# Storing a decoder block's result in pieces of 64 tokens instead of 32, and summing the first weights on GpSimd

## The chip, the cores and the metric

The kernel runs on one core of a Trainium2 chip. A core has TensorE (matmuls), VectorE, ScalarE and GpSimd, each with its own instruction stream, and SyncE (SP), which only issues DMAs; ScalarE can issue DMAs as well. In a profile they are PE (PEld for its weight loads), DVE, ACT, POOL and SP; SPq and ACTq are the issuing parts of two of them. Work on different engines is ordered by semaphores alone. The metric is the device time of one execution in microseconds, the median of several runs.

## What is computed

One block of a decoder for 512 tokens of width 2048 in float32: RMSNorm, one projection whose columns feed three token mixers (dilated attention, a convolution module, windowed attention), an output projection with residual, and then a SwiGLU feed-forward with residual:

```python
x = x + mix @ w_out[l]
h2 = _rms_norm(x, norm2_g[l])
x = x + (jax.nn.silu(h2 @ w_gate[l]) * (h2 @ w_up[l])) @ w_down[l]
```

The feed-forward is 5632 wide. The change lies in it alone.

## The kernel before

Every matrix product is done in three passes of a rounded type: each operand is split into a high half (rounded, on ScalarE) and a low half (the rest, on VectorE), and high x high, high x low and low x high are added. Gate and up (class `Wide`, 22 pairs of feature tiles) and down (class `Down`) also use a fast scheme for 2 x 2 blocks with seven products instead of eight, so that sums of weight blocks and sums of activation blocks have to be made.

*Weights.* A group of four blocks "11", "12", "21", "22" of gate and up is loaded by SP into raw buffers. `group` lists four additions per group (`add`, L184): s = 21 + 22, 21 += 11, s += 11, s += 12, each done in place once the split that reads the old value has been issued. They run on GpSimd, but for the very first group, g0, whose sums run on VectorE. `split_up_to` then makes the halves, two products ahead: two ScalarE copies (L295 into PSUM, L296 the high half) and a VectorE subtraction (L267). Down's weights are split the same way at L283 to L285, with the blocks rearranged in eight runs of 128 as they are written.

*Activations for down.* `Wide.piece` splits a result for 256 tokens per product: a ScalarE copy (L1154) into columns 0 to 255 of a tile `a` and a VectorE subtraction (L1155) into the next 256. The tile goes to DRAM and is loaded again for down. In `Down`, 128 of these columns at a time are TensorE's stationary operand, so that columns 0 to 127 (a = 0) and 128 to 255 (a = 1) give two output tiles [128 tokens, 512 channels].

*Down.* Twelve blocks (`DOWN`), g alternating between the halves of the output channels; each has seven products, each in two steps. The partial sums `y` carry a key (g, i, k, a): channels 1024 i + 512 g on, tokens 256 k + 128 a on. `done` adds the products to them; blocks 10 (g = 1) and 11 (g = 0) are the last of their half. The order of the work around it is written by hand in two lists, `evacs` and `extras`: `later(n, ...)` puts a call n steps ahead, and each step runs the front of both. The program runs on each engine in that order.

*Results.* The output is wanted with channels in rows. `store` (L1241 to L1259) transposes a finished `y` tile in 32 x 32 blocks on VectorE (L1245) into a tile `zo` and issues four DMAs, one for each 32 partitions (L1252): 32 rows of 16 pieces of 32 tokens, 128 bytes a piece. All are on SP's queue, except in the last product of all (`tail` in `product`), which is cut into a = 0 and two halves of a = 1, whose stores alternate between SP and ScalarE's queue. Stores that stand in `extras` when the tail begins are issued after it, in the closing loop. The residual is loaded through `turned` in the same arrangement of tokens.

The framework gives DMAs of SP and ScalarE's queue eight completion semaphores in turn (DMAHW0 to 7 in the lists below); a DMA waits for the one that used its semaphore before.

Of the kernel before, what the change touches and what calls it, by code (L numbers as in the profile page):

```python
# [9 lines left out]
F32 = mybir.dt.float32  # L10
# [6 lines left out]
P = 128  # L17
# [99 lines left out]
def kernel(ctx: ExitStack, tc: tile.TileContext, xT, wi, wo, wgu, wd, cst_in, outT):  # L117
# [51 lines left out]
    def group(name, m, n, blocks):  # L169

        key = {k: (k, name) for k in ("11", "12", "21", "22", "s")}
        for k in ("22", "21", "11", "12"):
            entries.append((k + "ab"[m] if k[0] == "2" else k, key[k], blocks[k]))
        u = len(works)

        def add(to, a, b, last=None):
            def go():
                if to == a:
                    out = raws[key[to]][0]
                else:  # L180
                    out = take("s" + "ab"[m], key[to], n)

                eng = nc.vector if name == "g0" else nc.gpsimd
                eng.tensor_add(out[:, :n], raws[key[a]][0][:, :n], raws[key[b]][0][:, :n])  # L184
                if last:
                    drop(key[last])
            return go

        sums[u - 4].append(add("s", "21", "22"))
        sums[u - 3].append(add("21", "21", "11"))  # L190
        sums[u].append(add("s", "s", "11", "11"))
        sums[u + 2].append(add("s", "s", "12"))
        works.extend((key[k], last, None) for k, last in (
            ("s", False), ("11", False), ("21", True), ("s", False), ("12", True), ("22", True), ("s", True)))
# [15 lines left out]
    for t, (g, r) in enumerate(DOWN):  # L210
        first, end = RANGES[r]
        base = len(works)
        keys, size = {}, {}
        for c, (lo, hi) in {"A": (first, first + 2), "B": (first + 2, end)}.items():
            keys[c] = {k: (k, f"d{t}{c}") for k in ("11", "12", "21", "22", "s")}
            size[c] = 4 * P * (hi - lo)
            bufs[c]["12"] = bufs[c]["11"]
        for k in ("21A", "11A", "21B", "11B", "22A", "22B", "12A", "12B"):
            c = k[2]
            span = (first, first + 2) if c == "A" else (first + 2, end)  # L220
            entries.append((bufs[c][k[:2]], keys[c][k[:2]], [down_block(g, int(k[0]) - 1, int(k[1]) - 1, *span)]))

        def add(c, other, last=False, buf=None):
            key, n = keys[c], size[c]

            def go():

                out = raws[key["21"]][0] if buf is None else take(buf, key["s"], n)
                nc.gpsimd.tensor_add(out[:, :n], raws[key["21"]][0][:, :n], raws[key[other]][0][:, :n])
                if last:  # L230
                    drop(key[other])
            return go

        for i, c in enumerate("AB"):
            sums[base - 4 + i].append(add(c, "11", buf=bufs[c]["s"]))
            sums[base + i].append(add(c, "22"))
            sums[base + 3 + i].append(add(c, "11", last=True))
            sums[base + 7 + i].append(add(c, "12"))
        works.extend((keys[c][k], last, "moves") for k, last in (
            ("s", True), ("11", False), ("21", False), ("21", False), ("22", True), ("12", True), ("21", True)) for c in "AB")  # L240
        bufs = {c: {"21": b["s"], "s": b["11"], "11": b["22"], "22": b["21"]} for c, b in bufs.items()}

    splits = {}
# [797 lines left out]
    acts = {}  # L1041
    od = {p: tc.dram_tile([P, 7 * T], F32, name=f"od{p}") for p in range(NP)}
    evacs, extras = [], []
    flip = [1]

    def run(queue):
# [44 lines left out]
    class Wide(Block):  # L1091
# [55 lines left out]
        def piece(self, at, src):  # L1147
            n = src.shape[-1] // TH
            near = psum["high"].tile([P, 1024], F32R, name=f"{self.name}n{at}", tag="h")[:, :n * TH]
            nc.scalar.copy(near, src)  # L1150
            for k in range(n):
                q, s = LAID[at + k], slice(k * TH, (k + 1) * TH)
                t = slot(f"a{q}_{self.p}", F32R)
                nc.scalar.copy(t[:, :TH], src[:, s])  # L1154
                nc.vector.tensor_sub(t[:, TH:], src[:, s], near[:, s].bitcast(F32))  # L1155
                later(0, nc.sync.dma_start, od[self.p][:, (at + k) * T:(at + k + 1) * T], t.bitcast(F32), queue=extras)

        def piece1(self):
# [19 lines left out]
    def turned(dram, key, part):  # L1178

        g, i, k, a = key  # L1180
        c, t = 1024 * i + 512 * g, 256 * k + P * a + 32 * part
        return dram[c:c + T, t:t + 32].rearrange("(b i) t -> i b t", i=32)

    def by_blocks(t, part):
# [53 lines left out]
                load_next(3)  # L1238
            run(extras)

    def store(key, lo=0, hi=T, engs=(nc.sync,), now=False):  # L1241

        g, i, k, a = key
        z = slot("zo")
        nc.vector.transpose(z[:, lo:hi], y[key][:, lo:hi])  # L1245

        def go():
            out = outT.rearrange("n p t -> (n p) t")
            for part in range(4):
                c = 1024 * i + 512 * g  # L1250
                to = out[c + lo:c + hi, 256 * k + P * a + 32 * part:256 * k + P * a + 32 * part + 32]
                engs[part % len(engs)].dma_start(to.rearrange("(b i) t -> i b t", i=32),  # L1252
                                                 z[32 * part:32 * part + 32, lo:hi].rearrange("p (b j) -> p b j", j=32))
        if now:
            go()
        else:
            later(1, go, queue=extras)
        if hi == T:
            y.pop(key)  # L1259

    class Down:

# [9 lines left out]
        def product(self, k, q):  # L1272
# [13 lines left out]
            if tail:  # L1286

                out = banks + outs[:1]
                for n, (a, lo, hi) in enumerate(((0, 0, T), (1, 0, TH), (1, TH, T))):
                    self.multiply(q, out[n], units, a, lo, hi, True, True)  # L1290
                    key = self.sum(0, 1, a)
                    s = y[key][:, lo:hi]
                    nc.vector.tensor_add(s, s, out[n][:, lo:hi])
                    store(key, lo, hi, (nc.sync, nc.scalar), now=True)
                    if n == 0:
                        for b in range(2):
                            store(self.sum(0, 0, b), now=True)
                return
            if self.drops:
                for j in self.pairs:  # L1300
# [21 lines left out]
        def done(self, q, banks):  # L1322
            by = nc.vector
            for a, b in enumerate(banks):
# [12 lines left out]
                elif q == 4:  # L1337
                    self.add(1, 0, a, b, by)
                    if self.end:
                        later(0, store, self.sum(1, 1, a))  # L1340
                elif q == 2 and self.end:

                    t = slot(f"last{a}")
                    nc.scalar.copy(t, b)
                    self.add(0, 0, a, t, nc.gpsimd)
                    store(self.sum(1, 0, a))
                elif q == 2:
                    self.add(0, 0, a, b, by)
                else:
# [6 lines left out]
            if q == 3 and self.final:  # L1356
                for n, (i, k) in enumerate(((0, 0), (1, 1), (1, 0), (0, 1))):
                    for a in range(2):
                        later(2 * n + a, store, self.sum(i, k, a))

    blk = gate = None
    for t in range(len(DOWN)):
# [88 lines left out]
```

## Time and profile before

| | |
|---|---|
| median of 3 runs | 1904.18 us (1904.1 to 1905.18) |
| profiled execution, its own time | 1905.0 us |
| its span, first to last instruction | 1903.1 us |
| TensorE busy | 1874.6 us, 99% of the span |
| VectorE, ScalarE, GpSimd busy | 1466.9, 1347.0, 1057.3 us |
| stores of the result | 62 on SP, 6 on ScalarE's queue |

Rows of a timeline or group read: start and length in us (or busy and mean), engine, line, operation, output <- inputs, shape, count, and in brackets the idle time before it with what ended it. "SPq L1252 <- DMA out_T<-zo: 16.4, 4, 15.1" is a wait: who, for whom, us in total, times, longest. A window's row gives its length, each engine's busy time with the number of instructions, TensorE's granted clock, the mean busy share of the 16 DMA engines and GB/s.

### The profile page before, as it was taken

The numbers are of one execution on the slowest core, as the hardware profiler recorded it, in microseconds if no ns is written. First come the engines' busy times: TensorE is split into PE (matmuls) and PEld (weight loads), VectorE is DVE, ScalarE is ACT, GpSimd is POOL, SyncE is SP. The second block draws the span as 40 slices with busy tenths as digits, with TensorE's granted clock in tenths as the row PEclk, the third lists the DMA queues.
The fourth block names the chain that finished last, engine by engine and source line by source line (L and its number), as shares of the span: only waits on it lengthen the run. The fifth ranks groups of instructions, "written<-read, shape, count | busy, mean of one in ns | idle before, by whom it ended". The sixth has DMA issues, their size and how long they took to land.

```text
span 1903.1 us, 28403 instructions
## 1 busy us (share of the span) xinstructions
PE 1874.6 (99%) x9718; PEld 1603.6 (84%) x9718; DVE 1466.9 (77%) x2472; ACT 1347.0 (71%) x1869; POOL 1057.3 (56%) x662
## 2 busy tenths in 40 slices
PE   9999999999999999999999999999999999999994
PEld 7888888888888888888888888888888888888884
DVE  6789978998678777777778777777777777777774
ACT  6356654553467888888788888888788778777772
POOL 0111101000002887888787887887787878878773
PEclk9999999999999999999999999999999999999997
DMA  7232242333332445555456555554448857657435
GB/s 267 95 123 77 84 132 77 109 122 133 124 131 106 133 166 155 166 186 160 165 157 191 167 178 156 167 183 159 156 140 310 313 200 238 217 200 258 154 112 88
DMA packets 218785, 307.11 MB, mean 161 GB/s; under 512 B 80912, under 2 KB 130448, under 8 KB 218640
## 3 DMA queue, kind: packets, MB, share of 16 engines
q1 hardware_dynamic: 216352, 305.02, 49.5%
q8 instruction: 77, 1.26, 0.3%
q10 hardware_dynamic: 2288, 0.27, 0.1%
q14 instruction: 68, 0.56, 0.1%
HBM read 243.89 MB, written 52.95 MB: 156 GB/s over the span
## 4 chain that ended last, share of the span: by engine, by line
PE 96%; DVE 1%; POOL 1%; DMA 1%; issue 0%; ACT 0%; SPq 0%; DVEq 0%; POOLq 0%
PE out L1076 45%; PE out L1311 7%; PE out L1312 7%; PE out L1310 7%; PE o L318 3%; PE o L319 3%; PE o L320 3%; PE cq L320 2%; PE cq L318 2%; PE cq L319 2%; PE av L318 1%; PE ak L318 1%; PE av L320 1%; PE aq L320 1%; PE aq L318 1%; PE ak L320 1%
## 5 line engine op out<-in xcount | busy, mean ns | idle before, releaser
L1076 PE MATMUL out<-h,wh 128*128 128x512 f32 x2464 | 589.4, 391 | 0.0
L1076 PEld LDWEIGHTS out<-h,wh 128*128 128x128 f32 x2464 | 453.4, 189 | 87.7
L1076 PEld LDWEIGHTS out<-h,wl 128*128 128x128 f32 x2464 | 316.6, 192 | 14.2 <-DVE n2v L433 2.2
L1076 PE MATMUL out<-h,wl 128*128 128x256 f32 x2464 | 320.6, 283 | 2.0 <-DVE n2v L433 2.0
L1311 PE MATMUL out<-wl,a 128*128 128x512 f32 x620 | 241.1, 389 | 0.4 <-DVE wl L285 0.4
L1312 PE MATMUL out<-wh,a 128*128 128x512 f32 x620 | 240.4, 388 | 0.0
L1310 PE MATMUL out<-wh,a 128*128 128x512 f32 x620 | 240.4, 388 | 0.0
L289 ACT CAST wh<-w 128x1024 fp32r<-128x1024 f32 (+2 forms) x94 | 96.7, 1030 | 123.4 <-PE o L319 54.6
L267 DVE TENSOR_TENSOR wl<-w,wh 128x1024 fp32r<-128x1024 f32 (+2 forms) x95 | 112.8, 1187 | 37.2 <-ACT wh L289 37.0
L1311 PEld LDWEIGHTS out<-wl,a 128*128 128x128 f32 x620 | 116.4, 188 | 26.3 <-DVE wl L285 2.5
L1310 PEld LDWEIGHTS out<-wh,a 128*128 128x128 f32 x620 | 116.4, 188 | 24.2
L1312 PEld LDWEIGHTS out<-wh,a 128*128 128x128 f32 x620 | 116.4, 188 | 23.5
L1320 DVE TENSOR_TENSOR y<-y,out 128x512 f32<-128x512 f32 x164 | 106.3, 684 | 32.9 <-PE out L1312 20.8
L529 DVE SCALAR_TENSOR_TENSOR y<-bu,cst,y 128x511 f32<-128x511 f32 (+14 forms) x120 | 87.6, 730 | 0.4
L434 POOL TENSOR_TENSOR n2r<-n2v,nhalf 128x4 f32<-128x4 f32 x1 | 2.0, 2030 | 109.5 <-DVE n2v L433 109.5
L318 PE MATMUL o<-mh_c,wh 128*128 128x512 f32 x128 | 51.1, 399 | 0.0
L318 PE MATMUL cq<-hh,wh 128*128 128x512 f32 x128 | 51.1, 399 | 0.0
L320 PE MATMUL cq<-hh,wl 128*128 128x512 f32 x128 | 50.1, 391 | 0.0
L320 PE MATMUL o<-mh_c,wl 128*128 128x512 f32 x128 | 50.0, 391 | 0.0
L319 PE MATMUL cq<-hl,wh 128*128 128x512 f32 x128 | 50.0, 390 | 0.0
L319 PE MATMUL o<-ml_c,wh 128*128 128x512 f32 x128 | 49.9, 390 | 0.0
L434 POOL TENSOR_TENSOR lvr<-lvv,nhalf 128x4 f32<-128x4 f32 x1 | 1.9, 1921 | 74.5 <-DVE lvv L433 74.5
(3012 smaller groups left out, 4935.1 us busy)
## 6 DMA issues: line engine op xcount, KB each, us to landing
od<-a SPq DMA_DIRECT2D x154, 256.0 KB, 4.8
a<-od SPq DMA_DIRECT2D x154, 256.0 KB, 5.4
w<-in_wi SPq DMA_DIRECT2D x58, 512.0 KB, 3.6
w<-in_wo SPq DMA_DIRECT2D x32, 512.0 KB, 3.5
x<-in_xT SPq DMA_DIRECT2D x16, 256.0 KB, 6.9
xr<-in_xT SPq DMA_DIRECT2D x16, 256.0 KB, 3.7
x2d<-xr SPq DMA_DIRECT2D x16, 256.0 KB, 2.0
z<-x2d SPq DMA_DIRECT2D x64, 64.0 KB, 3.7
```

The source lines that it names most:

```text
L267: fn(*args)
L289: (nc.vector.tensor_copy if u == 0 else nc.scalar.copy)(hi[:, :n], t[:, :n])
L318: nc.tensor.matmul(out, wh, xh, start=start, stop=False)
L319: nc.tensor.matmul(out, wh, xl, start=False, stop=False)
L320: nc.tensor.matmul(out, wl, xh, start=False, stop=stop)
L434: nc.gpsimd.tensor_tensor(r, v, nhalf[:, :NT], op=ALU.pow)
L529: nc.vector.scalar_tensor_tensor(yconv[j][:, i:], hconv[j][:, :T - i], c, yconv[j][:, i:], op0=ALU.mult, op1=ALU.add)
L1076: nc.tensor.matmul(out, lhs[:, s], rhs, start=begin, stop=x is xs[-1] and low == flip[0], skip_group_check=True)
L1310: nc.tensor.matmul(b[:, lo:hi], x[:, high], wh[:, s], start=start, stop=False, skip_group_check=True)
L1311: nc.tensor.matmul(b[:, lo:hi], x[:, high], wl[:, s], start=False, stop=False, skip_group_check=True)
L1312: nc.tensor.matmul(b[:, lo:hi], x[:, low], wh[:, s], start=False, stop=last, skip_group_check=True)
L1320: getattr(eng, op)(t, t, src)
```

## The change

It has three parts. The tokens of a 256-token group are dealt to the two tiles in turns of 32: tile a takes tokens 64 b + 32 a + j for b = 0 to 3 and j = 0 to 31, so L1154 and L1155 write and read eight runs of 32 (`by_turns`, `by_tiles`), and the residual is loaded accordingly. The two tiles' transposes then write side by side into one tile per pair (`turn_back`), and one DMA for each 32 partitions stores 64 tokens in a piece, 256 bytes (`put`). These tiles take buffers of weights that the last block has used up. Third, g0's sums move to GpSimd.

```diff
@@ add in group
-                eng = nc.vector if name == "g0" else nc.gpsimd
-                eng.tensor_add(out[:, :n], raws[key[a]][0][:, :n], raws[key[b]][0][:, :n])
+                nc.gpsimd.tensor_add(out[:, :n], raws[key[a]][0][:, :n], raws[key[b]][0][:, :n])
...
+        final_bufs = bufs
         bufs = {c: {"21": b["s"], "s": b["11"], "11": b["22"], "22": b["21"]} for c, b in bufs.items()}
...
+    def by_turns(x):
+        return x.rearrange("p (b a j) -> p b a j", a=2, j=32)
+
+    def by_tiles(x):
+        return x.rearrange("p (a b j) -> p b a j", a=2, j=32)
@@ Wide.piece
-                nc.scalar.copy(t[:, :TH], src[:, s])
-                nc.vector.tensor_sub(t[:, TH:], src[:, s], near[:, s].bitcast(F32))
+                nc.scalar.copy(by_tiles(t[:, :TH]), by_turns(src[:, s]))
+                nc.vector.tensor_sub(by_tiles(t[:, TH:]), by_turns(src[:, s]), by_turns(near[:, s].bitcast(F32)))
@@ turned
-        c, t = 1024 * i + 512 * g, 256 * k + P * a + 32 * part
+        c, t = 1024 * i + 512 * g, 256 * k + 64 * part + 32 * a
@@ in place of store
+    pairs_out, engines = {}, [nc.sync, nc.scalar]
+
+    def turn_back(key, lo=0, hi=T):
+        g, i, k, a = key
+        if (g, i, k) not in pairs_out:
+            c = "AB"[len(pairs_out) % 2]
+            name = "22" if g == i == 0 else "s"
+            pairs_out[g, i, k] = wp.tile([P, 1024], F32, name=f"z{g}{i}{k}", tag=f"raw{final_bufs[c][name]}", bufs=1)
+        z = pairs_out[g, i, k].rearrange("p (b a j) -> p a b j", a=2, j=32)[:, a, lo // 32:hi // 32]
+        nc.vector.transpose(z, y[key][:, lo:hi].rearrange("p (b j) -> p b j", j=32))
         if hi == T:
             y.pop(key)
+
+    def put(g, i, k, lo=0, hi=T, engs=(nc.sync,)):
+        out, z = outT.rearrange("n p t -> (n p) t"), pairs_out[g, i, k]
+        c = 1024 * i + 512 * g
+        for part in range(4):
+            to = out[c + lo:c + hi, 256 * k + 64 * part:256 * k + 64 * part + 64]
+            engs[part % len(engs)].dma_start(to.rearrange("(b i) t -> i b t", i=32),
+                                             z[32 * part:32 * part + 32, 2 * lo:2 * hi].rearrange("p (b j) -> p b j", j=64))
@@ Down.product, the tail
-                    store(key, lo, hi, (nc.sync, nc.scalar), now=True)
+                    if n == 0:
+                        put(self.g, 1, 0)
...
+                    turn_back(self.sum(0, 1, a), lo, hi)
                     if n == 0:
                         for b in range(2):
-                            store(self.sum(0, 0, b), now=True)
+                            turn_back(self.sum(0, 0, b))
+                        put(self.g, 0, 0, engs=engines)
+                    else:
+                        put(self.g, 0, 1, lo, hi, engines)
@@ Down.done
-                        later(0, store, self.sum(1, 1, a))
+                        later(0, turn_back, self.sum(1, 1, a))
...
-                    store(self.sum(1, 0, a))
+                    turn_back(self.sum(1, 0, a))
+                    if a == 0:
+                        put(self.g, 1, 1)
...
-                        later(2 * n + a, store, self.sum(i, k, a))
+                        later(2 * n + a, turn_back, self.sum(i, k, a))
+                    later(2 * n + 2, put, self.g, i, k, queue=extras)
```

TensorE's list of instructions is the same, word for word. GpSimd's list around the start of gate and up, before (lvr and n2r are small steps of two norms):

```order
L434 TENSOR_TENSOR lvr<-lvv,nhalf 128x4
L434 TENSOR_TENSOR n2r<-n2v,nhalf 128x4
L184 TENSOR_TENSOR w('s', 'u0')_6059<-w('21', 'u0')_5736,w('22', 'u0')_5734 128x1024
L184 TENSOR_TENSOR w('21', 'u0')_5736<-w('21', 'u0')_5736,w('11', 'u0')_5984 128x1024
L1109 TENSOR_TENSOR g0r<-g0r,g0u 128x256
```

and with the change:

```order
L433 TENSOR_TENSOR lvr<-lvv,nhalf 128x4
L182 TENSOR_TENSOR w('s', 'g0')_5681<-w('21', 'g0')_5527,w('22', 'g0')_5525 128x1024
L182 TENSOR_TENSOR w('21', 'g0')_5527<-w('21', 'g0')_5527,w('11', 'g0')_5581 128x1024
L182 TENSOR_TENSOR w('s', 'g0')_5681<-w('s', 'g0')_5681,w('11', 'g0')_5581 128x1024
L433 TENSOR_TENSOR n2r<-n2v,nhalf 128x4
L182 TENSOR_TENSOR w('s', 'g0')_5681<-w('s', 'g0')_5681,w('12', 'g0')_5684 128x1024
L182 TENSOR_TENSOR w('s', 'u0')_6059<-w('21', 'u0')_5736,w('22', 'u0')_5734 128x1024
```

Three of g0's sums stand ahead of n2r, the fourth between n2r and the sums of the next group.

SP's list at its end, before. The first two rows are the last of the store ahead of the wait that the prediction speaks of, then come the eight held stores of g = 1, of which the first five are shown, and the first of the tail's own; 13 more of the tail's and 16 of earlier keys follow:

```order
L1252 DMA out_T<-zo 32x16x32 [waits DMAHW7_49]
L1252 DMA out_T<-zo 32x16x32 [waits DMAHW2_49]
L1252 DMA out_T<-zo 32x16x32 [waits DMAHW3_49,DVE_49]
L1252 DMA out_T<-zo 32x16x32 [waits DMAHW4_49]
L1252 DMA out_T<-zo 32x16x32 [waits DMAHW5_49]
L1252 DMA out_T<-zo 32x16x32 [waits DMAHW6_49]
L1252 DMA out_T<-zo 32x16x32 [waits DMAHW7_49,DVE_49]
...
L1252 DMA out_T<-zo 32x16x32 [waits DMAHW3_49,DVE_49]
```

and SP's whole list from the last pair but three on with the change (z_19027 is the pair i = 1, k = 1 of g = 0, z_19051 is 1, 0, z_19080 is 0, 0 and z_19078 is 0, 1):

```order
L1268 DMA out_T<-z_19027 32x16x64 [waits DMAHW2_49]
L1268 DMA out_T<-z_19051 32x16x64 [waits DMAHW4_49,DVE_49]
L1268 DMA out_T<-z_19051 32x16x64 [waits DMAHW7_49]
L1268 DMA out_T<-z_19051 32x16x64 [waits DMAHW1_49]
L1268 DMA out_T<-z_19051 32x16x64 [waits DMAHW2_49]
L1268 DMA out_T<-z_19080 32x16x64 [waits DMAHW3_49,DVE_49]
L1268 DMA out_T<-z_19080 32x16x64 [waits DMAHW4_49]
L1268 DMA out_T<-z_19078 32x8x64 [waits DMAHW5_49,DVE_49]
L1268 DMA out_T<-z_19078 32x8x64 [waits DMAHW6_49]
L1268 DMA out_T<-z_19078 32x8x64 [waits DMAHW7_49,DVE_49]
L1268 DMA out_T<-z_19078 32x8x64 [waits DMAHW0_49]
```

ScalarE's list at its end with the change:

```order
L1358 COPY last_19057<-out_5942 128x512 [waits PE_49]
L1268 DMA out_T<-z_19080 32x16x64 [waits DMAHW7_49,DVE_49]
L1268 DMA out_T<-z_19080 32x16x64 [waits DMAHW1_49]
L1268 DMA out_T<-z_19078 32x8x64 [waits DMAHW3_49,DVE_49]
L1268 DMA out_T<-z_19078 32x8x64 [waits DMAHW5_49]
L1268 DMA out_T<-z_19078 32x8x64 [waits DMAHW6_49,DVE_49]
L1268 DMA out_T<-z_19078 32x8x64 [waits DMAHW0_49]
```

The semaphores are dealt in one sequence over both lists: 7 goes to ScalarE's first store and then to the second store of z_19051, 1 to ScalarE's second and then to the third, 3 to ScalarE's third and then to the first store of z_19080, and so on to the end. Before, 3 went to ScalarE's second store and then to the third row of SP's list above.

More of the change, by code (lines that the diff above doesn't have):

```diff
@@ L1239 @@
             run(extras)
-    def store(key, lo=0, hi=T, engs=(nc.sync,), now=False):
+    pairs_out, engines = {}, [nc.sync, nc.scalar]
+    def turn_back(key, lo=0, hi=T):
         g, i, k, a = key
[L1244 to L1257, printed above, removed]
+        if (g, i, k) not in pairs_out:
[4 more added lines that the diff above has]
+        nc.vector.transpose(z, y[key][:, lo:hi].rearrange("p (b j) -> p b j", j=32))
         if hi == T:
             y.pop(key)
+    def put(g, i, k, lo=0, hi=T, engs=(nc.sync,)):
[5 more added lines that the diff above has]
+                                             z[32 * part:32 * part + 32, 2 * lo:2 * hi].rearrange("p (b j) -> p b j", j=64))
     class Down:
@@ L1290, in product @@
                     self.multiply(q, out[n], units, a, lo, hi, True, True)
-                    key = self.sum(0, 1, a)
-                    s = y[key][:, lo:hi]
-                    nc.vector.tensor_add(s, s, out[n][:, lo:hi])
-                    store(key, lo, hi, (nc.sync, nc.scalar), now=True)
+                    if n == 0:
+                        put(self.g, 1, 0)
+                    t = y[self.sum(0, 1, a)][:, lo:hi]
+                    nc.vector.tensor_add(t, t, out[n][:, lo:hi])
+                    turn_back(self.sum(0, 1, a), lo, hi)
                     if n == 0:
                         for b in range(2):
-                            store(self.sum(0, 0, b), now=True)
+                            turn_back(self.sum(0, 0, b))
+                        put(self.g, 0, 0, engs=engines)
+                    else:
+                        put(self.g, 0, 1, lo, hi, engines)
                 return
```

## The prediction

> **What bounds the kernel now.** I read the chain of waits first, then the last 40 us of each queue's timeline, then the one idle stretch of TensorE. The chain:
>
> ```profile
> PE 96%; DVE 1%; POOL 1%; DMA 1%; issue 0%; ACT 0%; SPq 0%; DVEq 0%; POOLq 0%
> ```
>
> TensorE sets the pace of nearly everything, and the change leaves its instructions as they are. So only time in which TensorE does not run can be won: the end, and a gap. The end, from the timelines of TensorE, VectorE and the two issuing queues, SP's waits, the account of the store's line and a window on the stores alone (columns there: length, busy of the five engines, clock, DMA share, GB/s):
>
> ```profile
> 1878.17 0.28 PE L1312 MATMUL out<-wh,a 128*128 128x256 f32 x1
> 1872.07 1.29 DVE L1245 STREAM_TRANSPOSE zo<-y 128x512 f32<-128x512 f32 x2
> 1876.41 1.90 DVE L1245 STREAM_TRANSPOSE zo<-y 128x512 f32<-128x512 f32 x3
> 1879.44 0.45 DVE L1245 STREAM_TRANSPOSE zo<-y 128x256 f32<-128x256 f32 x1
> 1877.16 3.88 ACTq L1252 DMA_DIRECT2D out_T<-zo  x6
> 1855.92 8.47 SPq L1252 DMA_DIRECT2D out_T<-zo  x14
> 1879.58 21.11 SPq L1252 DMA_DIRECT2D out_T<-zo  x38
> 1892.04 8.65 SPq L1252 DMA_DIRECT2D out_T<-zo  x16
> SPq L1252 <- DMA out_T<-zo: 16.4, 4, 15.1
> DMA to landing us min/median/max: 1.6/2.0/4.3
> 1892.00:1900.00 8.00, 0.00 (x0) 0.00 (x0) 0.00 (x0) 0.00 (x0) 0.00 (x0) 0.50 0.73 112
> ```
>
> TensorE ends at 1878.45 and VectorE's last transpose at 1879.89, but the span ends at 1903.1. In between SP issues 38 stores one after the other, 21.11 / 38 = 0.556 us each, and the last landing and the program's end take the 2.4 us from 1900.69 to 1903.1. Issue is the bound there: the DMA engines are busy for 0.73 of the window. Before that SP stood still for 15.1 us, from 1864.4 to 1879.5, held by a DMA of the same line: each issue first waits for the DMA that last used its completion semaphore (eight of them, shared by SP and ScalarE's queue), and the store on which SP stood has the semaphore of ScalarE's second tail store, which could not start before the last sums. SP went on 2.4 us after ScalarE's first store: half a microsecond of issue and a landing of 2.0. So eight stores of results long ready were held there, the tail's own 14 came behind them, and then 16 more of ready results.
>
> The gap, in the timelines of TensorE, ScalarE, VectorE and GpSimd around the start of gate and up:
>
> ```profile
> 603.31 1.11 PE L1076 MATMUL out<-h,wl 128*128 128x256 f32 x8
> 606.39 1.92 PE L1076 MATMUL out<-h,wl 128*128 128x256 f32 x8 [1.97 <-DVE n2v L433]
> 600.18 0.40 ACT L975 CAST h<-h 128x256 fp32r<-128x256 f32 x1
> 603.99 1.02 ACT L295 CAST wn<-w('s', 'g0')_5681 128x1024 fp32r<-128x1024 f32 x1 [3.41 <-DVE w('s', 'g0')_5681 L184]
> 586.31 1.22 DVE L267 TENSOR_TENSOR wl<-w('s', 'g0')_5681,wn 128x1024 fp32r<-128x1024 f32 x1
> 601.61 1.22 DVE L267 TENSOR_TENSOR wl<-w('21', 'g0')_5527,wn 128x1024 fp32r<-128x1024 f32 x1
> 602.74 1.22 DVE L184 TENSOR_TENSOR w('s', 'g0')_5681<-w('s', 'g0')_5681,w('11', 'g0')_5581 128x1024 f32<-128x1024 f32 x1
> 605.04 1.22 DVE L267 TENSOR_TENSOR wl<-w('s', 'g0')_5681,wn 128x1024 fp32r<-128x1024 f32 x1 [1.08 <-ACT wn L295]
> 606.42 2.03 POOL L434 TENSOR_TENSOR n2r<-n2v,nhalf 128x4 f32<-128x4 f32 x1 [109.48 <-DVE n2v L433]
> 608.42 2.39 POOL L184 TENSOR_TENSOR w('s', 'u0')_6059<-w('21', 'u0')_5736,w('22', 'u0')_5734 128x1024 f32<-128x1024 f32 x1
> 614.28 1.01 ACT L295 CAST wn<-w('s', 'u0')_6059 128x1024 fp32r<-128x1024 f32 x1
> ```
>
> TensorE stands for 1.97 us. The row names n2v, but what its product needs is the low half that VectorE finishes at 606.26, just before n2v. That waits for ScalarE's rounding at 603.99, which waited 3.41 us for VectorE's sum of 602.74. The sum stands in VectorE's order behind the work of the output projection. GpSimd sat idle for 109 us.
>
> **The change, part by part.** Sums are made against the profiled execution: span 1903.1, own time 1905.0, which is 0.8 above the median of 1904.18; I take the same saving off the median.
>
> *Sums of the first gate group to GpSimd.* Four additions leave VectorE. The one that matters has its operands when VectorE has read the first s, at 587.5; on GpSimd such a sum takes 2.39 us, so it is done by 590, ten us before ScalarE, free at 600.58, wants it. Then ScalarE rounds at 600.6 to 601.6, VectorE goes from 601.61's row straight to this low half and ends at about 604.0, and TensorE has its last matmul before the gap running until then. The 1.97 us go: **-2.0**. What is late next: GpSimd's fourth sum, queued between n2r and u0's first sum. Both start 2 us earlier, since n2v does, so u0's sum would end near 611.2, where it now ends at 610.8. ScalarE reads it at 614.3 now and 612.3 then; 1.1 us are left. Bounds: nothing (another wait takes over) to -2.2.
>
> *Pieces of 64 tokens.* A store now carries 32 rows x 16 pieces of 256 bytes, not 128. For all 68 stores of before (62 on SP, six on ScalarE's queue) there are now 36: 30 on SP, six on ScalarE's queue. Before, 38 of SP's came after 1879.5. By the new order 21 precede the first one that shares a semaphore with ScalarE's tail stores: four pairs of g = 1 and, as sums become ready, pair (1,1) and the first store of (1,0). All have data by about 1873.4, when the two transposes of 1872.07 end, and leave while TensorE works. Nine are left. The first of them waits for the landing of ScalarE's first tail store. That one follows the third transpose, whose end is 1878.31, so it goes at 1878.35 and lands 2.0 us later, at 1880.35. Nine issues at 0.556 take 5.0: the last issue ends at 1885.35, where it ended at 1900.69. The other stores of ScalarE's queue that these nine also wait for go at about half a microsecond's distance and land before SP's turn (the sixth at some 1883.5, SP's ninth being due at 1884.8). Saved: **-15.3**.
>
> What a 256-byte piece costs has no row. Issue: the rows with 512 pieces of 128 bytes take 0.55 us. If issue goes by pieces it stays at that; if by bytes it doubles to 1.1. Below nothing is excluded, since a store has no fewer pieces. I take 0.556. On the DMA engines a store now takes 0.73 x 0.55 = 0.40 us; after, 0.40 (by pieces) to 0.80 (by bytes). Seven full and eight half stores fall into the tail, 11 full ones' worth, 4.4 to 8.8 us against 7.0 from ScalarE's first store to SP's last issue. Between the two: gate and up moves 168 GB/s at a share of 0.53 (row below), 317 at a full one, in pieces of kilobytes; at that rate 64 KB take 0.20, which leaves 0.20 for 512 short pieces, so 128 KB in as many take 0.41 + 0.20 = 0.61. Eleven are 6.7 us: the engines just keep up, and I leave the sum to issue.
>
> The Trainium skill ("DMA: Bandwidth & Descriptors", section "Why small descriptors are slow (HBM only)") gives a descriptor a fixed overhead of 3 cycles beside one for every 32 bytes. By that rule 256 bytes cost 11 cycles and 128 cost 7, an estimate of 0.63 us a store, 6.9 us in all; the sum would stay as it is, only just. The same page (section "Issuing engines are not separate DMA queues") speaks against the second queue: several issuers save only the sequencer's time, which it calls usually small. Here the trace disagrees with "small": 0.55 of issue against 0.40 of engine. By the rule ScalarE's six stores would save nothing; fifteen in one file from 1878.35 would end at 1886.7, and the sum would be 1.3 us worse.
>
> *Transposes.* They write 16 runs of 32 now. No row shows this; the nearest are two lines of the down stage that write eight runs of 128, beside a plain copy and 605.04's plain subtraction of the same size:
>
> ```profile
> L283 ACT CAST wn<-w('21', 'd0A')_14842 x3: 1005/1010/1022, 1462.5 to 1483.4; 128x1024 fp32r<-128x1024 f32 x3
> L295 ACT CAST wn<-w('s', 'g0')_5681 x3: 1007/1017/1020, 582.3 to 612.4; 128x1024 fp32r<-128x1024 f32 x3
> L285 DVE TENSOR_TENSOR wl<-w('21', 'd0A')_14842,wn x3: 1214/1214/1222, 1465.0 to 1485.4; 128x1024 fp32r<-128x1024 f32 x3
> ```
>
> Runs cost nothing there, so I take 0; the bound is twice the time, +1.9 for the three on the path. A gain has no source.
>
> *Copies by turns.* 154 roundings on ScalarE (L1154) and 154 subtractions on VectorE (L1155) now read and write eight runs of 32. By the same rows: 0. Cover, in a stretch of gate and up, for all engines and for L1154 alone:
>
> ```profile
> 700.00:1400.00 700.00, 700.00 (x4028) 618.73 (x4027) 534.15 (x790) 580.18 (x738) 560.72 (x360) 1.00 0.53 168
> 700.00:1400.00 700.00, 45.59 (x126) 1.00 0.53 168
> ```
>
> ScalarE is idle for 119.8 us, 0.95 per copy of 0.36; VectorE for 165.9. Without that cover 0.1 us more per copy would cost 15 us.
>
> *The reused buffers.* The results' tiles now take the place of finished weights, each used twice or thrice, so a transpose waits for stores, and behind it on VectorE stand low halves for TensorE. The tightest is pair (0,1) of g = 1, behind pair (1,1)'s stores, which now come after the second load of 12:
>
> ```profile
> 1853.71 0.76 SPq L252 DMA_DIRECT2D w('12', 'd11B')_18875<-in_wd  x1
> 1859.83 0.69 DVE L1245 STREAM_TRANSPOSE zo<-y 128x512 f32<-128x512 f32 x1
> ```
>
> The load goes some 0.6 us earlier than now, the four stores after it are issued by about 1855.8 and land by 1857.8, or 1859.6 at the longest landing seen (4.3 from issue). The transpose comes at 1859.83: 0.
>
> Sum: -2.0 - 15.3 = -17.3: span 1885.8, own time 1887.7, median **1886.9**.
>
> **Rivals.** *Bytes decide on the DMA engines* (0.80 a store). 8.8 us from 1878.35 end at 1887.15, where the forecast's issue ends at 1885.35: 1.8 later, 1888.7. For it: no row shows pieces of 256 bytes. Against: the 317 GB/s of large pieces beside the 112 / 0.73 = 153 of short ones; by bytes alone they would be equal.
>
> *Bytes decide at issue*, 1.1 us each: nine stores end 5 us later, 1891.9. Against: the load of 512 KB at 1853.71 was issued in 0.76.
>
> *The gap stays*, because ScalarE or GpSimd is late with something else: 1888.9. Against: the 10 us of slack of the sum.
>
> *The change does not free SP.* The shared semaphores hold all 14 stores of the last four pairs, not nine: five more at 0.556, 1889.7. For it: exactly this stood for 15.1 us. Against: the new order's waits name long landed stores for these five.
>
> *Slower: the copies by turns make ScalarE the bound of gate and up.* Place: L1154, 154 copies. It decides from 0.36 + 0.95 = 1.31 us a copy on; 0.11 us beyond that, 1.42, eats the whole gain. At four times the price, 1.45, it costs 0.14 x 154 = 21.6 and gives 1908.5. For it: eight short runs per copy, twice over. Against: the L283 row, which has as many runs and no cost.
>
> **How the numbers follow.** Forecast 0.66 (1885 to 1888.3: transposes, landings and the engines' share). Engines by bytes 0.13, gap stays 0.08, SP held again 0.05, issue by bytes 0.03, slower 0.02; the rest, 0.03, is a tail shorter than I reckon, because landings are quicker or the issue of fewer rows is. The range 1884.4 to 1890.8 takes in all but the last two rivals and the ends of the unknown costs. Faster by more than 0.2% (3.8 us; about what can be told from no change): all but the slower case and a percent or two of mishaps in it, 0.96; same 0.02, slower 0.02.
>
> **What would show it.** Right: SP's row of out_T stores after TensorE's end has 9, not 38, at 0.55 each, the first 2.0 us after ScalarE's first; the span ends about 9.3 us after TensorE's last matmul, where it was 24.7. TensorE's wait of 1.97 at the third product's successor is gone and its last matmul ends near 1876.4. L1154 keeps its 0.36 us. Wrong: a DMA share near 1 in the tail (engines by bytes), 1 us between issues (issue by bytes), ScalarE over 95% in gate and up (slower), a wait of VectorE's transposes for out_T, or more than nine stores behind ScalarE's first.

## The result and the profile after

The changed kernel takes 1886.51 us (median of 5 runs, 1886.18 to 1886.97), beside 1904.1 us for the kernel before on the same chip (1903.15 to 1905.18): a ratio of 0.9908, 95% interval 0.9893 to 0.9922. That is 17.6 us less; the forecast was 17.3 less. The profiled execution took 1886.69 us, its span 1884.7, which is 18.4 less than the span before. The sum came out well because two terms missed in opposite directions, so the two places are shown apart.

First the end of the span, from the timelines of TensorE, VectorE, ScalarE's queue and SP in the changed kernel (start, length, engine, line):

```profile
1874.17 0.28 PE L1326 MATMUL out<-wh,a 128*128 128x256 f32 x1
1872.41 1.90 DVE L1258 STREAM_TRANSPOSE z<-y 128x512 f32<-128x512 f32 x3
1875.43 0.45 DVE L1258 STREAM_TRANSPOSE z<-y 128x256 f32<-128x256 f32 x1
1874.34 3.01 ACTq L1268 DMA_DIRECT2D out_T<-z  x6
1876.75 5.64 SPq L1268 DMA_DIRECT2D out_T<-z  x9
```

TensorE ends at 1874.45 and the span at 1884.7. These 10.25 us, which I call the tail, were 24.65 before and 9.3 in the forecast. SP has nine stores behind ScalarE's first, as foretold. But the first of them comes 2.41 us after ScalarE's first, not 2.0, and the nine take 0.63 us each, not 0.556. SP's waits, the stores' times to landing and a window on the nine stores (length, busy time of five engines, clock, share of the DMA engines, GB/s) say why:

```profile
SPq L1268 <- DMA out_T<-z: 7.0, 2, 6.7
```

```profile
out_T<-z ACTq DMA_DIRECT2D x2, 128.0 KB, 2.5
out_T<-z ACTq DMA_DIRECT2D x4, 64.0 KB, 2.1
```

```profile
1876.70:1882.40 5.70, 0.00 (x0) 0.00 (x0) 0.00 (x0) 0.00 (x0) 0.00 (x0) 0.65 0.99 188
```

A store of 128 KB lands in 2.5 us where one of 64 KB takes 2.1; the forecast had used the 2.0 of the 64 KB stores of before. And the DMA engines are busy for 0.99 of the window: at 188 GB/s a store of 128 KB takes 0.70 us of theirs. In this stretch they are the bound, and no longer the issue. SP still stands for 6.7 us, held by ScalarE's first tail store.

Second the start of gate and up, in the timelines of TensorE, ScalarE, VectorE and GpSimd with the change:

```profile
603.18 2.07 PE L1083 MATMUL out<-h,wl 128*128 128x256 f32 x16
605.09 2.00 PE L1083 MATMUL out<-h,wh 128*128 128x512 f32 x8
606.93 0.60 PE L366 MATMUL r2s<-ident,n2r 128*128 128x128 f32 x4
600.35 1.01 ACT L294 CAST wn<-w('s', 'g0')_5681 128x1024 fp32r<-128x1024 f32 x1
602.60 1.22 DVE L266 TENSOR_TENSOR wl<-w('s', 'g0')_5681,wn 128x1024 fp32r<-128x1024 f32 x1
587.53 2.45 POOL L182 TENSOR_TENSOR w('s', 'g0')_5681<-w('s', 'g0')_5681,w('11', 'g0')_5581 128x1024 f32<-128x1024 f32 x1 [16.77 <-DVE wl L266]
607.32 2.40 POOL L182 TENSOR_TENSOR w('s', 'u0')_6059<-w('21', 'u0')_5736,w('22', 'u0')_5734 128x1024 f32<-128x1024 f32 x1
```

The sum starts at 587.53 on GpSimd, ScalarE rounds at 600.35, VectorE's low half ends at 603.82 and TensorE does not stand. All this is as forecast. Yet the small transposes of r2s, which came 7.53 us after the start of the first of these matmuls (603.31 to 610.84), now come 3.75 us after it: 3.8 us are gone where the gap was 1.97. The kernel before has a second loss there that I had not read. Two windows of its trace, the first one with the gap in it:

```profile
603.23:606.64 3.41, 1.44 (x12) 1.20 (x11) 2.31 (x4) 2.65 (x3) 0.22 (x1) 0.99 0.43 132
606.64:610.05 3.41, 3.41 (x13) 3.02 (x13) 3.38 (x5) 3.13 (x4) 3.41 (x2) 0.51 0.06 22
```

After the gap TensorE's granted clock is 0.5 for 3.41 us. The changed kernel keeps a clock of 1.00 through this stretch.

The copies by turns cost nothing. L1161 (before L1154) takes 45.16 / 125 = 0.361 us, before 0.362, and the transposes into 16 runs average 693 ns, before 692:

```profile
700.00:1400.00 700.00, 45.16 (x125) 1.00 0.56 168
```

```profile
L1258 DVE STREAM_TRANSPOSE z<-y 128x512 f32<-128x512 f32 x15 | 10.1, 693 | 0.0
```

### The profile page after: what moved, and what is told of

Read it like the earlier page. It is cut to its first block, busy times and chain, and to the rows that moved or that the text cites. A ratio compares the mean times of both kernels' runs of the same rounds, so it can differ in the third digit from the quotient of the medians.

```text
span 1884.7 us, 28337 instructions
## 1 busy us (share of the span) xinstructions
PE 1872.2 (99%) x9718; PEld 1601.8 (85%) x9718; DVE 1468.5 (78%) x2468; ACT 1346.3 (71%) x1869; POOL 1065.3 (57%) x666
## 4 chain that ended last, share of the span: by engine, by line
PE 98%; DMA 1%; POOL 0%; DVE 0%; issue 0%; SPq 0%; ACT 0%; DVEq 0%; POOLq 0%
PE out L1083 45%; PE out L1325 7%; PE out L1326 7%; PE out L1324 7%; PE o L319 3%; PE o L318 3%; PE o L317 3%; PE cq L319 2%; PE cq L317 2%; PE cq L318 2%; PE av L317 1%; PE ak L317 1%; PE aq L319 1%; PE av L319 1%; PE ak L319 1%; PE aq L317 1%
```

## The experiments

They ask two things: what the front's gap costs and why, and which part of the change made the tail shorter. "Tail" is always the time from TensorE's last matmul to the end of the span in the profiled execution.

### The first group's sums alone

One part of the change undone:

```diff
-                nc.gpsimd.tensor_add(out[:, :n], ...)
+                eng = nc.vector if name == "g0" else nc.gpsimd
+                eng.tensor_add(out[:, :n], ...)
```

> The changed kernel with one part undone: the first gate group's four sums are on VectorE again. Theory A (the prediction's term): the gap costs its idle time alone, 2.0 us, so 1888.5 us. Theory B: the gap also makes the granted TensorE clock fall to a half for some 3.4 us after it, as it did in the trace before; then it costs 3.9 us in all, 1890.4 us, and a window of 606.4 to 608.1 us shows a clock near 0.5. The tail is to stay as it is in both, about 10.2 us from TensorE's end to the span's.

Measured: 1889.79 us (4 runs, 1888.6 to 1890.24; ratio to before 0.9926, 0.9911 to 0.9941), against 0.9908 for the whole change: 0.0018, or 3.4 us. This interval and that of the whole change overlap, so the comparison would not settle it by itself. The gap of 1.97 us is back at 604.40 and the tail is 10.2 us. But the clock does not fall in this execution:

```profile
602.43:605.84 3.41, 1.97 (x13) 1.60 (x11) 2.33 (x3) 1.87 (x2) 0.00 (x0) 1.00 0.20 43
605.84:609.25 3.41, 2.88 (x16) 2.37 (x16) 3.39 (x6) 3.41 (x5) 2.85 (x2) 1.00 0.27 111
```

So theory B, as I had put it, is wrong: the same gap at the same place does not always halve the clock. In the profiled execution TensorE ends 2.9 us later than with the whole change, more than A's 2.0. TensorE's list is the same in both, so its matmuls can be compared one by one: they start 0.1 us later ahead of the gap and 2.5 behind it. So 2.4 us are lost at the gap, where the kernel before loses 3.8; the other 0.5 lies elsewhere.

The converse: the kernel before with these sums on GpSimd and nothing else changed.

```diff
-                eng = nc.vector if name == "g0" else nc.gpsimd
-                eng.tensor_add(out[:, :n], ...)
+                nc.gpsimd.tensor_add(out[:, :n], ...)
```

> The kernel before with this one part of the change alone: the first gate group's sums on GpSimd, results stored as before. Theory A (idle time alone): 1902.1 us. Theory B (idle time and halved clock): 1900.2 us, with no window of half clock around 606 us. The tail is to stay at 24.65 us after TensorE's end in both.

Measured: 1900.69 us (10 runs), before 1904.06 on the same chip (19 runs): ratio 0.9981 (0.9972 to 0.999), 3.4 us less, and here the interval is clear of 1. Both comparisons put this part at 3.4 us, between A's 2.0 and B's 3.9. There is no gap and no half clock, and the tail is 24.6 us as before:

```profile
602.00:606.00 4.00, 4.00 (x27) 3.61 (x26) 3.97 (x7) 3.77 (x4) 2.52 (x2) 1.00 0.01 2
606.00:610.00 4.00, 4.00 (x26) 3.53 (x25) 3.43 (x6) 2.97 (x6) 3.92 (x3) 1.00 0.55 154
```

### Gaps of other lengths at the same place

Why does a gap of 1.97 us halve the clock in one execution and not in another? The trace's clock records give a hint: the clock rises some 5 us after the start (at 5.9 in the profile of before, at 5.1 in that of the sums on VectorE) and every stretch of one clock up to the end of the work is a whole number of 3.413 us (600.75, 3.41 and 1273.17 in before). So there are windows of fixed length whose edges fall differently in each execution. The windows above are cut at these edges. In before, the whole gap lies in one window and TensorE works 1.44 us of 3.41; with the sums on VectorE the edge falls inside the gap, and the two halves hold 1.97 and 2.88 us of work.

The next runs make gaps of other lengths by dummy sums on VectorE, just ahead of the low half that TensorE needs. The first two ask only whether any stop lowers the clock:

```diff
+                if name == "g0" and last == "11":
+                    scratch = wp.tile([P, 2], F32, name="scratch", tag="scratch", bufs=1)
+                    for _ in range(2):   # or 3
+                        nc.vector.tensor_reduce(scratch[:, :1], raws[key["12"]][0][:, :512], ...)
                 nc.gpsimd.tensor_add(out[:, :n], ...)
```

> The changed kernel with two dummy sums over 512 columns put on VectorE just ahead of the low half on which TensorE stood before: a gap of about 0.7 us at the same place by another cause. Theory A (any stop of TensorE lowers the clock): the granted clock falls to 0.5 for some 3.4 us after it. Theory B (a stop has to be near 2 us): the clock stays at 1.0 and the cost is the gap alone.

> As the run with two dummy sums, with three: a gap of about 1.4 us. Theory A: half clock for some 3.4 us after it. Theory B: the clock stays at 1.0.

Measured: gaps of 0.95 and 1.67 us, and the clock stays at 1.0 after both (the second was cut by an edge, 0.80 and 0.87). So theory A of these two, by which any stop does it, is wrong. But the times were 1913.94 and 1914.5 us, 27 us above the changed kernel, for a delay of one or two. The section "The place of the buffers" is about that. The next three runs test the windows; in them the dummies write to a small tile that was there already:

```diff
-                    scratch = wp.tile([P, 2], F32, name="scratch", tag="scratch", bufs=1)
+                    dummy = cp.tile([P, 1], F32, name="dummy", tag="small", bufs=24)
```

> The changed kernel with four dummy sums over 512 columns on VectorE ahead of the same low half, written to a small tile that already exists, so that no buffer moves. By the 0.9 and 1.7 us that two and three of them gave, TensorE should stand for 2.4 us. Theory A (the clock is set by windows of 3.41 us, counted from its first rise; a window in which TensorE stands for more than half halves the clock in the next): the trace's own window edges tell it; half clock for 3.41 us if 1.9 us or more of the gap lie in one window, full clock if 1.5 or less do. Theory B (a gap never does it, the half clock before had another cause): clock 1.0 throughout. Apart from the gap the kernel is to be as fast as the changed one, about 1889 to 1891 us, if moved buffers were what made the runs with two and three dummies 27 us slower; if the dummies did it, it comes out near 1914 us again.

> The same with five dummy sums, a gap of about 3.2 us. Theory A: half clock after the window that holds 1.9 us or more of it, which one of two windows does unless the edge falls near the gap's middle. Theory B: clock 1.0. Time about 1890 to 1892 us.

> The same with seven dummy sums, a gap of about 4.7 us. Theory A: however the edges fall, one window holds at least 2.3 us of it, so the clock is halved after it for 3.41 us or twice that. Theory B: clock 1.0. Time about 1892 to 1894 us.

Measured: 1889.99, 1888.95 and 1893.2 us (one run each), with gaps of 2.42, 3.14 and 4.58 us. Windows cut at each execution's own edges, for four, five and seven dummies:

```profile
603.59:607.00 3.41, 0.99 (x8) 0.91 (x8) 3.38 (x6) 1.52 (x3) 0.89 (x1) 0.99 0.00 0
607.00:610.41 3.41, 3.41 (x11) 2.73 (x10) 3.34 (x5) 0.99 (x2) 3.41 (x3) 0.50 0.03 7
```

```profile
602.13:605.54 3.41, 1.88 (x13) 1.51 (x11) 3.27 (x6) 2.00 (x2) 0.00 (x0) 1.00 0.00 0
605.54:608.96 3.42, 1.82 (x12) 1.69 (x13) 3.42 (x6) 1.91 (x2) 1.79 (x2) 1.00 0.01 2
608.96:612.37 3.41, 3.41 (x19) 2.81 (x18) 3.19 (x6) 1.78 (x4) 3.41 (x2) 1.00 0.23 38
```

```profile
603.00:606.40 3.40, 1.08 (x9) 0.88 (x7) 3.23 (x6) 1.51 (x2) 0.00 (x0) 1.00 0.00 0
606.40:609.80 3.40, 1.14 (x5) 1.14 (x6) 3.37 (x6) 1.23 (x2) 1.11 (x2) 0.50 0.00 0
609.80:613.30 3.50, 3.50 (x12) 2.92 (x12) 3.11 (x5) 0.77 (x1) 3.50 (x2) 0.51 0.11 16
```

The second number of a row is TensorE's busy time, the third from the end the clock. With five dummies the gap is 3.14 us long, yet an edge cuts it into 1.54 and 1.60, each window has over 1.8 us of work, and the clock stays. With four it is shorter, 2.42, but lies in one window, 0.99 us of work, and the next window runs at half clock. With seven, two windows in a row are short of work and two run at 0.5. Every window with 0.99 to 1.44 us of work was followed by half clock, every one with 1.82 us or more by full clock; half of 3.41 is 1.71. Theory A holds in all three; B, by which a gap never does it, fails with four and with seven. The time with five is 1 us below the expected 1890 to 1892.

The ends of the executions agree with the rule. The last window in which TensorE works holds 0.71 to 1.49 us of work in eight of them, and half clock follows; in the others it holds 1.76 us or more, and the next window is still at full clock.

What the half clock costs is read from the rows between the gap's end and r2s. Before they take 606.39 to 610.84, 4.45 us; with the sums on VectorE and full clock, from the same gap's end, 606.37 to 609.43, 3.06 us. So it is 1.4 us. With the gap's 1.97 that makes 3.4 of the 3.8 us in the two profiles. The other 0.4 is lost without half clock too: it is the difference between the 2.4 us lost with the sums on VectorE and the gap's 1.97.

As a gap of 1.97 us only sometimes lies far enough in one window, the medians' 3.4 us are a mean over executions with this loss (3.8) and without it (2.4). Two of three profiled executions with this gap show it. The mean clock of the other executions bears this out. One window at half clock takes 0.5 x 3.41 / 1903 = 0.0009 off the mean. By the rule half clock sets in 1.7 to 5.1 us behind TensorE's end, as the edges fall; of the kernel before's 24.65 us that leaves 19.5 to 22.9, which take 0.0051 to 0.0060. So a mean clock of 0.993 means an execution with the loss and 0.995 one without; 0.994 can be either. Of the 33 executions of the kernel before that ran beside the experiments, five show 0.993 and take 1904.7 us in the mean, seven show 0.995 and take 1903.4: 1.3 us between them, where the rows above give 1.4.

The Trainium skill ("TensorE: Matmul & The Clock Gate", section "Part 1: The HAM clock gate (the "warmup" mystery)") states a free-running window of 3413 ns that does not reset when a kernel starts. The traces agree, with stretches of 3.41 us and edges that differ from run to run. Its section "HAM oscillation — how this bites in real kernels" gives the rule that gaps of over about 3.4 us do harm. There the measurement differs: gaps of 1.97 and 2.42 us did harm when they lay in one window. That 3.14 us across an edge did none fits both.

### The place of the buffers

The runs with four to seven dummies and no new tile took 1889 to 1893 us, so dummies alone do not cost 27 us. The changed kernel with one unused tile, one tiny fill of it, and no dummies:

```diff
+                if name == "g0" and last == "11":
+                    unused = wp.tile([P, 2], F32, name="unused", tag="unused", bufs=1)
+                    nc.vector.memset(unused, 0.0)
```

> The changed kernel with one unused tile of 8 bytes per partition ahead of the tiles of 2 KB that hold TensorE's stationary operands, which puts each of these 32 bytes further on (the allocator rounds to 32); no dummy work but one tiny fill. Theory A (the place of the operands made the runs with two and three dummies slower): 27 us slower, about 1913 us, the 512-column matmuls at 234 ns from start to start instead of 227. Theory B (the dummies or the chip did it): 1886.5 us.

Measured: 1912.64 us (4 runs, 1912.42 to 1912.82; ratio to before 1.0048, 1.0031 to 1.0064). Theory A: the 27 us of the two runs with a tile of their own came from this tile. It stands ahead of the 73 tiles of 2 KB, among them TensorE's operands. That it moves these by 32 bytes, from starts that are multiples of 64 to starts that are not, is worked out from the allocation; no trace shows the addresses. TensorE's timeline in the middle of gate and up, of the changed kernel and then of this one:

```profile
1000.78 3.82 PE L1083 MATMUL out<-h,wh 128*128 128x512 f32 x16
1004.44 2.08 PE L1083 MATMUL out<-h,wl 128*128 128x256 f32 x16
1006.35 3.82 PE L1083 MATMUL out<-h,wh 128*128 128x512 f32 x16
```

```profile
1000.64 2.03 PE L1086 MATMUL out<-h,wl 128*128 128x256 f32 x16
1002.51 3.89 PE L1086 MATMUL out<-h,wh 128*128 128x512 f32 x16
1006.24 2.03 PE L1086 MATMUL out<-h,wl 128*128 128x256 f32 x16
```

From start to start 16 matmuls of 512 columns take 3.66 us in the one and 3.73 in the other, 16 of 256 columns 1.91 and 1.87. The wide ones become slower by 2%, the narrow ones faster by 2%, and there is far more time in the wide ones. That the tile does it is shown; that the place is the reason is argued, and why it would be is not settled.

### The tail, part by part

The kernel before with all stores on SP. SP's stores then share no semaphore with ScalarE's queue:

```diff
-                    store(key, lo, hi, (nc.sync, nc.scalar), now=True)
+                    store(key, lo, hi, now=True)
```

> The kernel before with the tail's stores all on SP, none on ScalarE's queue; pieces, order and the first group's sums as before. Theory A (the hold by shared semaphores was a cost of its own): SP does not stand for 15.1 us, the eight held stores leave while TensorE works, 36 are left from 1877.2 us on, 36 x 0.556 = 20.0, plus 2.4: the span ends at 1899.6 instead of 1903.1, so 1900.6 us. Theory B (the hold cost nothing, since the DMA engines or SP's issue had no room before the tail anyway): six more stores in SP's file, 3.3 us more, 1907.5 us.

Measured: 1899.15 us (10 runs; ratio 0.9977, 0.9967 to 0.9986), 4.9 us less than before, and a tail of 20.3 us instead of 24.65. SP's stores of the tail:

```profile
1876.61 19.20 SPq L1252 DMA_DIRECT2D out_T<-zo  x36
```

There are 36, at 0.533 us each, and they start 1.30 us ahead of TensorE's end, where SP's 38 of before started 1.13 behind it. Theory A: the hold was a cost of its own, 4.4 us of tail, though SP had six more stores to issue.

The changed kernel with its stores cut in two, in the same order and from the same buffers:

```diff
-            to = out[c + lo:c + hi, 256 * k + 64 * part:256 * k + 64 * part + 64]
-            engs[part % len(engs)].dma_start(to..., z[32 * part:32 * part + 32, 2 * lo:2 * hi]...)
+            for a in range(2):
+                t = 256 * k + 64 * part + 32 * a
+                engs[part % len(engs)].dma_start(out[c + lo:c + hi, t:t + 32]..., z[...]...[:, a])
```

> The changed kernel with its 64-token stores cut in two again: the same order and buffers, but two DMAs with pieces of 32 tokens (128 bytes) for each with 64. By the order of the semaphores SP is held at pair 1,0's first store until ScalarE's second tail store has landed, and 20 stores are then left to SP, 12 go by ScalarE's queue. Theory A (issue is the bound of the tail, 0.556 us a store): 1877.1 + 20 x 0.556 + 2.3 = 1890.5, so 5.8 us slower than the changed kernel, 1892.3 us. Theory B (the DMA engines are the bound): 24 stores' worth of 64 KB at the 153 GB/s of 128-byte pieces take 10.3 us from 1874.4 on, plus 2.3: 1887.0, so 2.3 us slower, 1888.8 us.

Measured: 1892.11 us (4 runs; ratio 0.9935, 0.9918 to 0.9951), 5.6 us above the changed kernel, with a tail of 16.35 us. SP and a window on it after ScalarE's last store:

```profile
1875.88 12.37 SPq L1269 DMA_DIRECT2D out_T<-z  x20
```

```profile
1879.40:1888.20 8.80, 0.00 (x0) 0.00 (x0) 0.00 (x0) 0.00 (x0) 0.00 (x0) 0.50 0.66 100
```

Twenty stores, 8.3 us less tail than before, and the engines at 0.66: with 128-byte pieces issue is the bound (A), not the DMA engines (B). So of the 14.4 us by which the tail fell, 8.3 come from the new order alone, in which ready results have left before the end, and 6.1 from the larger pieces: SP issues 11 stores fewer, 5.64 us of issuing instead of 12.37. The division is rough, since SP's hold differs too: its file starts 1.7 us behind TensorE's end here and 2.3 in the changed kernel.

The changed kernel with the tail's stores on SP alone:

```diff
-    pairs_out, engines = {}, [nc.sync, nc.scalar]
+    pairs_out, engines = {}, [nc.sync]
```

> The changed kernel with the tail's stores all on SP, none on ScalarE's queue. Theory A (the prediction's sentence on a single file: fifteen issues one after the other from ScalarE's first store on): 1.3 us slower, 1887.8 us. Theory B (the second queue does harm, because SP's stores share its completion semaphores and stand until its stores have landed): pair 1,0's four stores leave at 1869.4 to 1871.6 us, four whole and eight half stores are left from 1874.34 us on, 12 x 0.556 = 6.7, last issue end 1881.0, plus 2.3 for the last landing: the span ends at 1883.3, 1.4 us sooner, 1885.1 us, and SP's wait of about 7 us for a DMA of the same line is gone.

Measured: 1885.6 us (4 runs; ratio 0.9904, 0.9888 to 0.9921). By the timing alone that is not told apart from the changed kernel, but the tail is 8.94 us, 1.3 less, near B's 1.4, and SP has no row of waits for a DMA of its own line any more:

```profile
1874.45 6.68 SPq L1268 DMA_DIRECT2D out_T<-z  x12
```

```profile
1874.40:1881.10 6.70, 0.16 (x2) 0.00 (x0) 1.52 (x5) 0.00 (x0) 0.00 (x0) 0.71 0.78 137
```

Twelve stores at 0.557 us with the engines at 0.78. Eight of them carry only 64 KB but are issued no faster, 0.55 us each, so this file is bound by issue. The second queue brought less than its hold on SP cost.

From these follows a version that should beat both kernels. VectorE is idle for 2.34 us before the last sums; there pair 0,0 can be transposed and stored. All stores go to SP, and pair 0,1 leaves in four whole stores at the end:

```diff
                     if n == 0:
                         put(self.g, 1, 0)
+                        for b in range(2):
+                            turn_back(self.sum(0, 0, b))
+                        put(self.g, 0, 0)
                     t = y[self.sum(0, 1, a)][:, lo:hi]
                     nc.vector.tensor_add(t, t, out[n][:, lo:hi])
                     turn_back(self.sum(0, 1, a), lo, hi)
-                    if n == 0:
...
-                    else:
-                        put(self.g, 0, 1, lo, hi, engines)
+                put(self.g, 0, 1)
```

> The changed kernel with pair 0,0 transposed and stored ahead of the last sums instead of behind the first of them (VectorE stands idle there for 2.34 us), all stores on SP, and pair 0,1 stored in four whole stores after the last transpose. Theory A (the tail is as long as the stores left behind the last sums take on the issue and the DMA engines): four stores from 1875.93 on, 0.70 us each by the engines' rate, 1878.7, plus 2.0: the span ends at 1880.7, 4.0 us sooner, 1882.5 us. Theory B (the time after TensorE's end is latency of the chain add, transpose, store, landing and the program's end, whatever the number of stores): no change, 1886.5 us.

Measured: 1882.66 us (4 runs, 1881.99 to 1883.97; ratio to before 0.9885, 0.9871 to 0.99), and a tail of 6.4 us, 3.9 less than the changed kernel's (A foretold 4.0):

```profile
1874.17 0.45 DVE L1258 STREAM_TRANSPOSE z<-y 128x256 f32<-128x256 f32 x1
1874.65 2.40 SPq L1268 DMA_DIRECT2D out_T<-z  x4
```

```profile
1870.00:1877.00 7.00, 3.61 (x28) 3.29 (x26) 3.80 (x7) 0.00 (x0) 0.08 (x1) 1.00 0.98 187
```

In this window every store is a whole one of 128 KB and all come from SP, and yet the engines are busy for 0.98 of it at 187 GB/s. So it is not the second queue that makes the engines the bound: one queue fills them with whole stores in a file, and half stores leave them partly idle.

It is the fastest version here, 22.0 us under the kernel before on the same chip by the medians. By the ratios, 0.9885 beside 0.9908, it is 4.4 us faster than the changed kernel.

## Why the prediction was right, point by point

**The bound.** It said that only time without TensorE can be won: the gap and the end. That held, but for one thing. TensorE can also run at half clock without showing a wait. The mean granted clock of before, 0.994, does not tell of the one window in which it did, since most of what it lacks is the idle end.

**The front, -2.0.** The mechanism was right in every step: the sum at 587.5, ScalarE at 600.35, the low half at 603.8 (reckoned 604.0), u0's sum at 609.7, 0.7 us before ScalarE read it (reckoned 1.1). The size was wrong: this part is worth 3.4 us by two comparisons. The step that failed is "The 1.97 us go: -2.0" with its bound of -2.2, which took a stop to cost its own length. Two rows that the prediction quotes showed it: 1.92 us for eight matmuls of 256 columns behind the gap, where 1.11 was the usual ahead of it.

**The tail, -15.3.** It fell by 14.4. Nine stores on SP, with the first held by ScalarE's first, came as worked out. Two terms of it were mis-sized: the landing (2.4 for 2.0, a store of double size) and the store (0.63 for 0.556 us, since the engines and not the issue set it). With them the end came 0.95 us later. Of the bounds on the DMA engines, 0.40 to 0.80 us a store, the estimate of 0.61 was taken; it is 0.70. "The engines just keep up" was therefore the wrong side of a near thing, and the rival in which bytes decide came half true: its sign, a share near 1 in the tail, appeared (0.99), at a price between the two. The rule of the Trainium skill weighed there ("DMA: Bandwidth & Descriptors", section "Why small descriptors are slow (HBM only)") gave an estimate of 0.63; the measured 0.70 is higher.

**The second queue.** The prediction held that ScalarE's six stores save 1.3 us against a single file. In the experiment the single file is 1.3 us shorter. What it left out is its own finding on the semaphores: without ScalarE's stores nothing holds SP, and the last three stores of pair 1,0 leave some 6 us sooner. The same page's section "Issuing engines are not separate DMA queues", on which it had let the trace decide, came nearer: more issuers brought nothing here.

**Costs set at nothing.** Copies, subtractions and transposes stayed within 0.002 us of their rows, and VectorE shows no wait for a store, so the reused buffers cost nothing. Issue did not double with the bytes: twelve stores in one file took 0.557 us each. Nor did it fall with the pieces, of which the half stores have half.

**The rivals.** "The gap stays", "the change does not free SP", "issue by bytes" and "slower" did not happen. The two misses, -1.4 at the front and +0.9 at the end, offset each other by luck; the median's 0.4 us from the forecast says nothing on the quality of either term.

## What to carry to other kernels

Price a short stop of TensorE by the clock as well as by its length: look at the granted clock in the windows right after it. Where two queues share completion semaphores, a late store on the one holds ready stores on the other, so try one queue, and send what is ready before the last result rather than behind it. After a change of buffers compare the start-to-start time of one kind of matmul, since one unused tile of 8 bytes cost more here than the whole edit brings.

## What was not expected of the hardware

- TensorE's clock is decided window by window, 3.41 us each, with edges that differ between executions. Windows with 0.71 to 1.49 us of work were followed by half clock, those with 1.76 us or more were not; between the two nothing was measured. The same gap of 1.97 us cost 1.4 us more or nothing more.
- One unused tile of 8 bytes ahead of the 2 KB tiles (by the allocation it moves them by 32 bytes, off multiples of 64) made 512-column matmuls 3.73 us per 16 instead of 3.66 and 256-column ones 1.87 instead of 1.91, and the kernel 26 us slower.
- Stores of 512 pieces of 256 bytes filled the DMA engines at 188 GB/s from two queues and at 187 from one, 0.70 us for 128 KB; with pieces of 128 bytes the rows of before give 112 / 0.73 = 153 GB/s.
